# Three small moves around the dilated attention of a hybrid encoder layer: a weight load eight filler steps later, three more filler steps ahead of the attention, and a unit's low part in front of later maxima

## The chip, the cores and the metric

The kernel runs on one core of a Trainium2 chip. Its time is the device time of one execution in microseconds (us). Three executions of the kernel before took 1283.53, 1284.01 and 1286.13 us, so the median is 1284.01 us. One more execution was profiled.

The core's engines are TensorE (PE in the rows; PEld is its loading of weights), VectorE (DVE), ScalarE (ACT), GpSimd (POOL) and SyncE (SP), which in this kernel only issues DMA transfers, one after the other in a fixed order. Rows that are marked SPq are transfers of that queue.

## The reference, cut to what matters

One encoder layer over a sequence of 1024 tokens and a model width of 1024, batch 1. A normed input is projected once, and the projection is cut into the inputs of two attentions and of two gates:

```python
def hybrid_layer(x, positions, attn_norm_g, w_in, b_gate, ...):
    h = rmsnorm(x, attn_norm_g)
    proj = h @ w_in
    (c_q, c_kv, k_rope, z_mla, q_dil, k_dil, v_dil, z_dil,
     g_mla, g_dil) = jnp.split(proj, split_points, axis=-1)
    a_out = mla_attention(c_q, c_kv, k_rope, positions, ...)
    y_mla = (a_out * jax.nn.silu(z_mla)) @ w_o_mla
    d_out = dilated_mixture(q_dil, k_dil, v_dil, positions)
    y_dil = (d_out * jax.nn.silu(z_dil)) @ w_o_dil
    gate_mla = jax.nn.sigmoid(g_mla + b_gate[:D_MODEL])
    gate_dil = jax.nn.sigmoid(g_dil + b_gate[D_MODEL:])
    merged = gate_mla * y_mla + gate_dil * y_dil
    return x + merged @ w_out
```

The dilated mixture has 24 heads of width 64 in three groups of eight. A query of group 0 sees its neighbours up to 64 tokens away, one of group 1 every fourth token up to 256 away, one of group 2 every sixteenth up to 1024 away. Head i of the three groups is combined into one output, by the softmax over the groups of the logarithms of their denominators:

```python
    for g, (window, dilation) in enumerate(DIL_CONFIGS):   # (128,1), (512,4), (2048,16)
        out, lse = dilated_group(q[:, :, sl], k[:, :, sl], v[:, :, sl], dilation, window // (2 * dilation))
        ...
    alpha = jax.nn.softmax(jnp.stack(lses, axis=0), axis=0)
    out = jnp.sum(alpha[..., None] * outs, axis=0)
```

The latent attention (8 heads, all tokens see all) is `mla_attention`. After the layer there is a last norm.

## The kernel before, in words

**Stages.** Up to about 460 us of the span the kernel norms the input, projects it and rotates queries and keys. Queries, keys and values go to buffers in DRAM (`s_dq`, `s_dk`, `s_dv`), from which the attentions load them in the layout they need. From about 460 to 813 us runs the dilated attention, then the latent attention, and last the output projections. Products in full precision are made of three passes, high by high, low by high and high by low part of the operands (`mm3`, lines 77 to 79 in the rows).

**Fillers.** The projections of the gates (24 weight tiles of 128 columns: `zs` and `gt`, the list `ZG`) are not a stage of their own. They are a generator, `fillers`, that is advanced by one step at a time wherever the attention leaves room on TensorE. A weight tile has two halves of 512 tokens, a half has eight steps, and a step is one `mm3`, three products of 128 by 512. With the first step of a tile's first half goes the load of the weights of the tile after the next (`self.wload`, a transfer `w_raw<-wt` of 512 KB, line 634), with its fifth step the rounding of the next tile's weights into two parts (line 636: ScalarE's `CAST w_h`, GpSimd's `w_l`). After a half the result goes through a scaling on VectorE (`zg_z`, line 617), a tanh on ScalarE (lines 619 and 624), for `zs` two operations on GpSimd (lines 620 and 621), and a store of 256 KB (`s_zs<-zg_t` or `s_gt<-zg_t`). These parts (`after`) are advanced one at a time with every other step of the next half.

**Units.** The dilated attention works on four pairs of heads. A pair has five items: two heads of group 0, two of group 1, and both heads of group 2 together (the classes). A head has four units of 256 queries, the classes have two, so there are 18 units a pair and 72 in all. A unit has eight parts, called by `do(t, part)`: 0 scores (`s_ps`, lines 860 and 861 on TensorE), 1 maxima (line 870 on VectorE, two a unit, which also write the masked scores to `p`), 2 exponentials (line 877 on ScalarE), 3 transposes of the probabilities (line 884 on TensorE, into `pt`) and their rounding (`pt_h`, line 892 on ScalarE), 4 the low part (`pt_l`, line 896 on VectorE: `pt` minus `pt_h`), 5 the products with the values (`av`, lines 908 and 915 on TensorE, with the high and with the low part), 6 and 7 the copying out and adding up (line 934 on VectorE). An item's queries and keys (`op_b`, `op_a`) are loaded two items ahead, its values (`op_c`) one unit later.

**The loop.** It runs over t, and different units are at different parts in one turn. After the first two items' loads come `FIRST_FEED` filler steps on their own, and then in each turn:

```python
            do(t, 3)
            do(t + 2, 0)
            do(t + 2, 1)
            do(t, 4)
            ...
            self.feed(DIL_FEED[g])
            do(t - 2, 6)
            do(t + 2, 2)
            do(t - 2, 7)
            self.feed(DIL_FEED[g])
            do(t - 1, 5)
```

So the scores, maxima and exponentials run two units ahead of the transposes, and the products with the values one unit behind these. `feed` advances the fillers by 1.43 steps on the average, twice a turn; over the whole loop that makes 273 steps. After the loop, steps are taken until a half tile is whole (`while not self.whole`).

**Combining a pair.** When the last unit of a pair is through, `combine` spreads nine pieces of work over the next turns: the statistics go to DRAM and come back by token (`s_sd`, `c_sn`), differences, exponents and quotients are formed (`c_w`, `c_d`, lines 1100 to 1121), these factors go to DRAM (`s_rr<-c_w`) and come back spread over 64 partitions (`bc<-s_rr`, twelve transfers, 256 KB for two of them), and VectorE multiplies the three groups' sums by them (the weighted sums, line 1134), while GpSimd adds them up. The first of the spread tiles have five buffers; the last two transfers wait for one to come free.

**What sets the order.** From the start of the dilated attention to its end the order of the instructions on TensorE, VectorE, ScalarE and GpSimd is that in which the program calls them (`manual_schedule`). Before and after it a scheduler places the instructions, and the transfers in SP's queue that belong to earlier work are placed by it among the first transfers of the attention. Each engine then works off its own order, and waits where the next instruction's inputs or buffers are not ready.

Of the kernel before, what the change touches and what calls it, by code (L numbers as in the profile page):

```python
# [27 lines left out]
QK_SCALE = float(np.float32(96.0 ** -0.5))  # L28


FIRST_FEED = 19
DIL_FEED = (1.43, 1.43, 2.5, 2)
FEED = (0.95, 0.95)

# [12 lines left out]
def run_all(gen):  # L47
    while True:
        try:
            next(gen)  # L50
        except StopIteration as e:
            return e.value


class Net:
# [546 lines left out]
    def fillers(self):  # L602
# [3 lines left out]
        with tc.tile_pool(name="zt", reuse_waits="tile", bufs=2, side="right") as tp:  # L606
            z_tile = lambda: tp.tile([128, 512], F32, name="zg_z")
            t_tile = lambda: tp.tile([128, 512], F32, name="zg_t")
            tiles = ZG
# [17 lines left out]
            for n, i in enumerate(tiles):  # L627
                w = ahead
                for half in range(2):
                    ps = self.pj.tile([128, 512], F32, name="pj")  # L630
                    t = slice(half * 512, half * 512 + 512)
                    for kc in range(8):
                        self.mm3(ps, *self.at(w, kc), self.hTh[:, kc, t], self.hTl[:, kc, t], kc == 0, kc == 7)
                        if half == 0 and kc == 0 and n + 2 < len(tiles):
                            raw.append(self.wload(src(n + 2)))
                        if half == 0 and kc == 4 and n + 1 < len(tiles):
                            ahead = self.wtile(None, raw=raw.pop(0))

                        if kc % 2 == 0 and self.tail:
                            next(self.tail, None)  # L640
                        self.whole = kc == 7
                        if kc < 7:
                            yield
                    if self.manual:
                        self.tail = after(i, half, ps)
                    else:
                        self.tail = run_all(after(i, half, ps))
                    if self.dil_done and todo:
                        j, h2 = todo.pop(0)
                        self.piece(self.da, j, h2, 4 + j, self.brd, z_tile(), t_tile())  # L650
                    yield
# [15 lines left out]
        for dt in range(8):  # L667
            if dt % 2 == 0:
                w = self.wtile(a["wod"][dt // 2])
            for half in range(2):  # L670
                c = slice(512 * half, 512 * half + 512)
                t, ps = yield from self.o_proj(1, dt, half, w, dt % 2 * 4, range(4), self.brd, t_tile(), self.pj)
# [11 lines left out]
        for dt in range(8):  # L684
            if dt % 2 == 0:
                w = self.wtile(a["wom"][dt // 2], n=6)
            for half in range(2):
                c = slice(512 * half, 512 * half + 512)
                t, ps = yield from self.o_proj(0, dt, half, w, dt % 2 * 3, range(3), self.brm, t_tile(), self.pj)
# [323 lines left out]
    def dil_attention(self, ap, dx, pp):  # L1013

        items, units, ends = [], [], {}
        for pair in range(4):
            st, nums = {}, {}
            for g in range(2):
                for hh in range(2):
                    items.append(self.dil_head(pair, g, hh, st, nums, ap, dx, pp))  # L1020
            items.append(self.dil_classes(pair, st, nums, ap, dx, pp))
            ends[len(items) - 1] = self.combine(pair, st, nums, ap, dx, pp)
        for n, it in enumerate(items):
            for k, x in enumerate(it[2]):
                units.append((*x, n if k == len(it[2]) - 1 else None))
        for it in items[:2]:
            it[0]()
            it[1]()
        later = {}
        N = len(units)  # L1030

        def do(k, what):
            if 0 <= k < N:
                units[k][1 + what]()
        for _ in range(FIRST_FEED):
            next(self.fill)
        for t in range(-2, N + 11):
            g = units[min(max(t, 0), N - 1)][0] if t <= N else 3
            do(t, 3)
            do(t + 2, 0)  # L1040
            do(t + 2, 1)
            do(t, 4)
            if t + 2 < N:
                last = units[t + 2][-1]
                if last is not None and last + 2 < len(items):
                    items[last + 2][0]()
# [6 lines that stand above are left out]
            if 1 <= t <= N:  # L1053
                last = units[t - 1][-1]
                if last is not None:
                    if last + 2 < len(items):
                        items[last + 2][1]()
                    for k, f in ends.get(last, {}).items():
                        later.setdefault(t + 1 + k, []).append(f)
            for f in later.pop(t, []):  # L1060
                f()
# [318 lines left out]
```

## Time and profile before

| What | Value |
|---|---|
| Median of three executions | 1284.01 us (1283.53 to 1286.13) |
| Profiled execution, its own time | 1285.26 us |
| Its span in the profile | 1283.4 us |
| Mean granted clock of TensorE | 0.988 of full |
| TensorE busy | 1235.9 us, 96% of the span |
| VectorE, ScalarE, GpSimd busy | 755.8, 608.1, 506.6 us |
| DMA engines, main queue | 218.17 MB, 60.3% of 16 engines' span |
| The dilated attention | from about 460 to 813 us |

The profiled execution's own time is 1.86 us longer than its span, which begins with the first and ends with the last instruction that the profiler saw. A row of the timeline has the start, the length, the engine, the line in the kernel, the operation, the tile written and the tiles read, the shape and, at the end, how many instructions of the same kind in a row it stands for. A bracket behind it has the time for which the engine stood idle before the first of them, and what ended that idle time, by the profile. The clock is the share of full speed that the chip granted to TensorE. DMA share is the mean busy share of the core's 16 DMA engines.

### The profile page before, as it was taken

The numbers are of one execution on the slowest core, as the hardware profiler recorded it, in microseconds if no ns is written. First come the engines' busy times: TensorE is split into PE (matmuls) and PEld (weight loads), VectorE is DVE, ScalarE is ACT, GpSimd is POOL, SyncE is SP. The second block draws the span as 40 slices with busy tenths as digits, with TensorE's granted clock in tenths as the row PEclk, the third lists the DMA queues.
The fourth block names the chain that finished last, engine by engine and source line by source line (L and its number), as shares of the span: only waits on it lengthen the run. The fifth ranks groups of instructions, "written<-read, shape, count | busy, mean of one in ns | idle before, by whom it ended". The sixth has DMA issues, their size and how long they took to land.

```text
span 1283.4 us, 19686 instructions
## 1 busy us (share of the span) xinstructions
PE 1235.9 (96%) x6957; PEld 1072.8 (84%) x6957; DVE 755.8 (59%) x1368; ACT 608.1 (47%) x1276; POOL 506.6 (39%) x402
## 2 busy tenths in 40 slices
PE   8989999999999989998999999999999999997998
PEld 8989999888888868887888888887888888884886
DVE  7473526566566635566575663655556666669632
ACT  6533336443433426555554642455556555454322
POOL 2351219887777624526231132311112111246522
PEclk9989999999999999999999999999999999999999
DMA  9957583276456586978889796445437444236421
GB/s 321 258 168 270 219 295 132 99 189 168 119 139 163 123 215 182 212 195 222 211 215 231 187 241 163 150 131 149 113 93 199 117 119 129 70 112 208 145 97 68
DMA packets 134482, 219.43 MB, mean 171 GB/s; under 512 B 37160, under 2 KB 66672, under 8 KB 130480
## 3 DMA queue, kind: packets, MB, share of 16 engines
q1 hardware_dynamic: 134384, 218.17, 60.3%
q8 instruction: 55, 0.90, 0.3%
q14 instruction: 43, 0.35, 0.1%
HBM read 149.37 MB, written 68.75 MB: 170 GB/s over the span
## 4 chain that ended last, share of the span: by engine, by line
PE 65%; DMA 10%; issue 5%; DVE 5%; POOL 4%; ACT 2%; SPq 1%; DVEq 0%; ACTq 0%; POOLq 0%
PE pj L77 9%; PE pj L79 9%; PE pj L78 9%; PE pt L754 4%; PE av L763 2%; PE s_mla L77 2%; PE av L762 2%; PE s_mla L78 2%; PE s_mla L79 2%; DMA bc<-s_rr 2%; PE st_c L79 2%; PE st_c L77 2%; PE st_c L78 2%; PE st_d L78 2%; PE st_d L79 2%
## 5 line engine op out<-in xcount | busy, mean ns | idle before, releaser
L84 POOL TENSOR_TENSOR w_l<-w_raw,w_h 128x512 fp32r<-128x512 f32 (+1 forms) x176 | 227.4, 1305 | 411.7 <-ACT w_h L83 354.7
L77 PE MATMUL pj<-hT_h,w_h 128*128 128x512 f32 x384 | 156.5, 408 | 0.0
L79 PE MATMUL pj<-hT_h,w_l 128*128 128x512 f32 x384 | 152.3, 396 | 0.0
L78 PE MATMUL pj<-hT_l,w_h 128*128 128x512 f32 x384 | 152.1, 396 | 0.0
L83 ACT CAST w_h<-w_raw 128x512 fp32r<-128x512 f32 (+1 forms) x176 | 104.3, 615 | 84.5 <-POOL w_raw L427 72.8
L84 DVE TENSOR_TENSOR pt_l<-pt,pt_h 128x512 fp32r<-128x512 f32 x128 | 87.9, 688 | 66.1 <-ACT pt_h L83 65.2
L83 ACT CAST pt_h<-pt 128x512 fp32r<-128x512 f32 x128 | 74.6, 585 | 79.6 <-PE pt L754 47.8
L77 PE MATMUL pj<-w_h,hT_h 128*128 128x256 f32 x384 | 109.7, 286 | 0.0
L78 PE MATMUL pj<-w_l,hT_h 128*128 128x256 f32 x384 | 109.5, 285 | 0.0
L79 PE MATMUL pj<-w_h,hT_l 128*128 128x256 f32 x384 | 109.3, 285 | 0.0
L740 DVE TENSOR_REDUCE m_nm<-s_mla 128x1 f32<-128x1024 f32 x64 | 78.2, 1222 | 26.7 <-PE s_mla L79 26.1
L870 DVE CUSTOM_DVE_ANT_0 p<-s_ps,masks 128x256 f32<-128x256 f32 x128 | 48.9, 419 | 69.8 <-PE s_ps L861 59.7
L877 ACT ACTIVATE p<-p,d_st 128x256 f32<-128x256 f32 x128 | 64.1, 502 | 51.3 <-DVE d_st L870 51.2
L79 PEld LDWEIGHTS pj<-hT_h,w_l 128*128 128x128 f32 x384 | 73.0, 190 | 15.9
L78 PEld LDWEIGHTS pj<-hT_l,w_h 128*128 128x128 f32 x384 | 73.3, 191 | 11.4
L77 PEld LDWEIGHTS pj<-hT_h,w_h 128*128 128x128 f32 x384 | 73.4, 191 | 11.2
L743 ACT ACTIVATE p<-s_mla,m_nm 128x1024 f32<-128x1024 f32 x64 | 71.8, 1122 | 18.2 <-PE pt L754 17.3
L754 PE MATMUL pt<-consts,p 128*128 128x128 f32 x512 | 78.1, 272 | 1.7 <-ACT p L743 1.7
L77 PEld LDWEIGHTS pj<-w_h,hT_h 128*128 128x128 f32 x384 | 74.2, 193 | 0.9
L78 PEld LDWEIGHTS pj<-w_l,hT_h 128*128 128x128 f32 x384 | 74.2, 193 | 0.8
L79 PEld LDWEIGHTS pj<-w_h,hT_l 128*128 128x128 f32 x384 | 74.2, 193 | 0.8
L762 PE MATMUL av<-pt_h,op_c 128*128 128x256 f32 x256 | 68.8, 289 | 0.0
(307 smaller groups left out, 3319.3 us busy)
## 6 DMA issues: line engine op xcount, KB each, us to landing
w_raw<-wt SPq DMA_DIRECT2D x48, 512.0 KB, 3.6
op_b<-s_dq SPq DMA_DIRECT2D x32, 512.0 KB, 8.0
gate<-s_gt SPq DMA_DIRECT2D x43, 256.0 KB, 3.0
s_dq<-dq_st SPq DMA_DIRECT2D x80, 128.0 KB, 2.4
s_dk<-dq_st SPq DMA_DIRECT2D x80, 128.0 KB, 2.4
s_dv<-dv_st SPq DMA_DIRECT2D x32, 256.0 KB, 4.3
s_gt<-zg_t SPq DMA_DIRECT2D x32, 256.0 KB, 3.8
w_raw<-wv SPq DMA_DIRECT2D x12, 512.0 KB, 5.2
```

Of the source, the lines that this page charges most:

```text
L77: mm(out, lh, rh, start=start, stop=False, skip_group_check=skip)
L78: mm(out, lh, rl, start=False, stop=False, skip_group_check=skip)
L79: return mm(out, ll, rh, start=False, stop=stop, skip_group_check=skip)
L83: self.nc.scalar.copy(out=h, in_=raw)
L84: sub.tensor_tensor(out=l, in0=raw, in1=h.bitcast(F32), op=ALU.subtract)
L740: v.tensor_reduce(out=nm[:, hh, qb:qb + 1], in_=s, axis=AX.X, op=ALU.max, negate=True)
L743: nc.scalar.activation(out=p, in_=s, func=AF.Exp, bias=nm[:, hh, qb:qb + 1], accum_out=den[:, hh, qb:qb + 1])
L754: self.anchor = nc.tensor.transpose(pt[:, o:o + 128], P[b2][:, 128 * kc:128 * kc + 128], self.ident)
L762: nc.tensor.matmul(a_out, vv[:, kc], ph[:, s], start=kc == 0, stop=False)
L763: nc.tensor.matmul(a_out, vv[:, kc], pl[:, s], start=False, stop=kc == 7)
L870: nc.vector.tensor_tensor_reduce(out=p[:, c], in0=x["s"][:, c], in1=mask, op0=ALU.add, op1=ALU.min, scale=-0.125, scalar=3e38, accum_out=s ...
L877: nc.scalar.activation(out=p, in_=p, func=AF.Exp, scale=-1.0, bias=nm, accum_out=den)
```

## The change

There are three edits.

- `FIRST_FEED` is 22 and no longer 19: three more filler steps stand ahead of the first unit's scores. All later filler steps stand three steps earlier against the units, which is about one turn of the loop (2 times 1.43 steps). The number of steps of the stage, 19 + 273 = 292, used to be filled up to 296 by four steps after the loop; now it is 22 + 273 = 295 and one.
- In `fillers` the load of the third tile's weights (n is 0 there, and `src(n + 2)` the third tile) goes with the first step of the first tile's second half, eight steps later. For all other tiles the condition says what it said.
- In the loop the low part of unit t (part 4) is called ahead of the maxima of unit t + 2 (part 1).

```diff
-FIRST_FEED = 19
+FIRST_FEED = 22
...
                     for kc in range(8):
                         self.mm3(ps, *self.at(w, kc), self.hTh[:, kc, t], self.hTl[:, kc, t], kc == 0, kc == 7)
-                        if half == 0 and kc == 0 and n + 2 < len(tiles):
+                        if half == (n == 0) and kc == 0 and n + 2 < len(tiles):
                             raw.append(self.wload(src(n + 2)))
                         if half == 0 and kc == 4 and n + 1 < len(tiles):
                             ahead = self.wtile(None, raw=raw.pop(0))
...
             do(t, 3)
             do(t + 2, 0)
+            do(t, 4)
             do(t + 2, 1)
-            do(t, 4)
```

Three places show what this makes of the order. The first is SP's queue around the start of the dilated attention, before the change and after it. `op_c` are the values of the second item, `w_raw` of the first such row is the load of the third tile's weights, `s_dk2` are the last stores of keys of the stage before, and `s_zs` the fillers' first store. The number behind a name is the buffer's.

```order
L73 DMA op_a_4807<-s_dk0_65 64x1152 x2
L73 DMA op_c_4812<-s_dv0_68 128x9x128
L73 DMA w_raw_4821<-wt 128x1024
L73 DMA s_dk2_67<-dq_st00_4743 32x1024 x4
L73 DMA s_dk2_67<-dq_st10_4744 32x1024 x4
L73 DMA s_zs_71<-zg_t_4857 128x512
L73 DMA w_raw_4888<-wt 128x1024
```

```order
L73 DMA op_a_4807<-s_dk0_65 64x1152 x2
L73 DMA op_c_4812<-s_dv0_68 128x9x128
L73 DMA w_raw_4854<-wt 128x1024
L73 DMA s_dk2_67<-dq_st00_4743 32x1024 x4
L73 DMA s_dk2_67<-dq_st10_4744 32x1024 x4
L73 DMA s_zs_71<-zg_t_4857 128x512
L73 DMA w_raw_4888<-wt 128x1024
```

The third tile's load is a later one by its number, but stands at the same place: behind the loads of the second item and ahead of the last eight stores of keys.

The second place is VectorE's order at the first units of the first head, before and after. The rows of line 870 are the maxima of a unit (two, each with the reading of its result), line 896 is a low part and line 617 a filler's scaling.

```order
L870 ISA p,d_st<-s_ps,masks 128x256
L870 ISA d_st 128x1
L870 ISA p,d_st<-s_ps,masks 128x256
L870 ISA d_st 128x1
L896 TENSOR_TENSOR pt_l<-pt,pt_h 128x512
L617 TENSOR_TENSOR zg_z<-pj,R 128x512
L870 ISA p,d_st<-s_ps,masks 128x256
```

```order
L617 TENSOR_TENSOR zg_z<-pj,R 128x512
L896 TENSOR_TENSOR pt_l<-pt,pt_h 128x512
L870 ISA p,d_st<-s_ps,masks 128x256
L870 ISA d_st 128x1
L870 ISA p,d_st<-s_ps,masks 128x256
L870 ISA d_st 128x1
L896 TENSOR_TENSOR pt_l<-pt,pt_h 128x512
```

The low part moved from behind the two maxima of the unit two further on to ahead of them, and the filler's scaling, three steps earlier, from behind the low part to one turn ahead.

The third place is SP's queue where the factors of the second pair are spread. The rows are a piece of the difference, `s_rr` are the factors on their way to DRAM, `bc` their spreading, and `w_raw` and `s_gt` belong to the fillers.

```order
 L73 DMA op_a<-s_dk_66 64x1024 x2
+L73 DMA s_gt<-zg_t 128x512
 L73 DMA s_rr<-c_w 16x6x64
-L73 DMA s_gt<-zg_t 128x512
+L73 DMA w_raw<-wt 128x1024
 L73 DMA bc<-s_rr 64x512 x10
-L73 DMA w_raw<-wt 128x1024
 L73 DMA op_c<-s_dv_69 128x8x128
 L73 DMA bc<-s_rr 64x512 x2
```

The fillers' store moved from behind the factors to ahead of them, and the fillers' weight load from behind the first ten spreading transfers to ahead of these. At the other pairs the fillers' stores and loads move by as much: at the first pair two stores and a weight load come ahead of the loads of the next items, at the third a weight load comes ahead of the loads of keys and a store ahead of the factors, and at the last a store comes between the first ten spreading transfers and the last two, with the weight loads around it earlier by one place.

## The prediction

> **What bounds the kernel now.** I read the page's busy shares, then the dilated stage by stretches, then TensorE's own idle time in that stage, row by row, and last the queues that end each wait.
>
> ```profile
> PE 1235.9 (96%) x6957; PEld 1072.8 (84%) x6957; DVE 755.8 (59%) x1368; ACT 608.1 (47%) x1276; POOL 506.6 (39%) x402
> 460.00:780.00 320.00, 303.79 (x1840) 267.97 (x1839) 188.62 (x491) 171.71 (x441) 111.02 (x100) 0.98 0.85 210
> ```
>
> TensorE sets the end: it is busy for 96% of the span. The second row (length, then busy time of PE, PEld, DVE, ACT, POOL, then the granted clock, the DMA share, GB/s) is the dilated stage, which all three edits touch: 320 us, of which PE works 303.8, so some 16 us are idle, while the DMA engines are 85% busy at 210 GB/s. The timeline of PE has that idle time in few places (start, length of the first, the work, and in brackets the idle time and what ended it):
>
> ```profile
> 480.24 1.18 PE L884 MATMUL pt<-consts,p 128*128 128x128 f32 x4 [5.48 <-ACT p L877]
> 590.70 0.38 PE L915 MATMUL av<-pt_l,op_c 128*128 128x256 f32 x1 [1.09 <-DVE pt_l L896]
> 600.32 0.38 PE L915 MATMUL av<-pt_l,op_c 128*128 128x256 f32 x1 [2.45 <-DVE pt_l L896]
> 674.46 0.39 PE L915 MATMUL av<-pt_l,op_c 128*128 128x256 f32 x1 [2.36 <-DVE pt_l L896]
> 691.42 0.36 PE L860 MATMUL s_ps<-op_a,op_b 128*128 128x256 f32 x1 [2.00 <-DMA op_a<-s_dk]
> 743.00 0.39 PE L915 MATMUL av<-pt_l,op_c 128*128 128x256 f32 x1 [1.59 <-DVE pt_l L896]
> 751.22 0.38 PE L915 MATMUL av<-pt_l,op_c 128*128 128x256 f32 x1 [1.05 <-DVE pt_l L896]
> ```
>
> These make 16.0 us: 5.5 before the first unit, and 10.5 around the three places where a pair of heads is combined. A stall also costs clock:
>
> ```profile
> 480.24:484.60 4.36, 4.36 (x14) 3.60 (x15) 2.40 (x8) 4.00 (x14) 3.87 (x4) 0.50 0.54 180
> 600.80:604.30 3.50, 3.50 (x15) 3.11 (x14) 2.97 (x11) 2.92 (x9) 0.45 (x1) 0.51 0.87 284
> 676.00:679.30 3.30, 3.30 (x10) 2.52 (x9) 3.30 (x12) 2.93 (x9) 1.04 (x2) 0.50 0.96 338
> 691.50:694.90 3.40, 3.40 (x17) 2.89 (x18) 2.03 (x6) 1.09 (x4) 0.84 (x1) 1.00 0.95 185
> ```
>
> After the stalls of 5.48, 2.45 and 2.36 us the clock is at a half for 4.36, 3.5 and 3.3 us, so 2.2, 1.7 and 1.7 us are lost; after the one of 2.00 us it stays at 1.00. All of it together, 16 + 5.6, is what can be won in this stage, and the edits aim at pieces of it.
>
> **The later load of the third tile.** In the queue of SP the load stands where it stood: behind the first six loads of the attention, ahead of the last eight stores of keys, in both programs. What it loads, when it may start and what waits behind it are the same. Its consumer, ScalarE's rounding at the fifth filler step of the second tile, is the same step too. So 0.
>
> **Three more steps ahead.** What ends the first stall:
>
> ```profile
> 457.25 0.39 PE L77 MATMUL pj<-hT_h,w_h 128*128 128x512 f32 x1
> 457.93 0.39 PE L77 MATMUL pj<-hT_h,w_h 128*128 128x512 f32 x1
> 465.79 10.80 SPq L73 DMA_DIRECT2D s_dk<-dq_st  x8
> 479.11 0.42 DVE L870 CUSTOM_DVE_ANT_0 p<-s_ps,masks 128x256 f32<-128x256 f32 x1 [10.10 <-DMA s_dk<-dq_st]
> ```
>
> One filler step takes 457.93 - 457.25 = 0.68 us, three take 2.04. The first maxima wait for the last stores of keys (their buffers lie where the probabilities go), which SP issues from 465.79 on for 10.8 us. Nothing in that chain is moved, so the units begin at 480.24 as before; the three steps run inside the stall, which falls from 5.48 to 3.44 us. The stage's number of steps is rounded up to whole half tiles: 19 + 273 = 292 became 296 with four steps of padding, 22 + 273 = 295 becomes 296 with one. So the 2.04 us come off at the end of the stage, and whether they are won is decided there:
>
> ```profile
> 809.71 0.69 DVE L1134 TENSOR_TENSOR num<-num,bc 128x512 f32<-128x512 f32 x1 [1.32 <-DMA bc<-s_rr]
> 810.92 2.54 DVE L740 TENSOR_REDUCE m_nm<-s_mla 128x1 f32<-128x1024 f32 x2
> 813.19 0.19 ACT L743 ACTIVATION_READ_ACCUMULATOR p<-s_mla,m_nm 128x1 f32 x1
> 813.43 0.44 PE L754 MATMUL pt<-consts,p 128*128 128x128 f32 x2
> ```
>
> The first transposes of the latent attention start 0.05 us after its first probabilities are ready (813.19 + 0.19), and these wait for VectorE, which comes straight from the last weighted sums of the last pair. PE, 2.04 us early, would stand and wait for them. What can come forward is that chain on VectorE, by as much as the filler's scalings in it no longer wait for PE; the order has one of them now ahead of the denominators, and on SP a gate store ahead of the last spreading, which ends the wait at 809.71; both take part of that back. I take -0.3, between -2.04 (chain fully earlier) and +1.25 (the store's 256 KB at the 210 GB/s above, in full).
>
> The clock at the start: 3.44 us is still longer than the stalls of 2.36 and 2.45 that halved it, so I take a loss of 1.7 in place of 2.2: -0.5, between -2.2 (no halving) and 0.
>
> The Trainium skill ("TensorE: Matmul & The Clock Gate", "Why this matters for your kernels") says to keep idle gaps of TensorE under about 3 us, since one idle window of some 3.4 us halves the clock. For this stall it agrees with what I took from the rows: 3.44 is still too long. For the stalls of 2.45 and 2.36 us the trace differs (0.51 and 0.50), and I go by the trace; by the page's limit the new short stalls below would cost no clock, and the sum would be -3.8 in place of -2.8.
>
> **The low part ahead of the maxima.** At the waits for pt_l VectorE comes late out of a weighted sum, and then works off its queue. At the second one:
>
> ```profile
> 598.90 0.41 DVE L870 CUSTOM_DVE_ANT_0 p<-s_ps,masks 128x256 f32<-128x256 f32 x1
> 599.59 0.68 DVE L896 TENSOR_TENSOR pt_l<-pt,pt_h 128x512 fp32r<-128x512 f32 x1
> 599.36 0.51 ACT L877 ACTIVATE p<-p,d_st 128x256 f32<-128x256 f32 x1 [4.12 <-DVE d_st L870]
> 599.86 0.49 ACT L877 ACTIVATE p<-p,d_st 128x256 f32<-128x256 f32 x1
> 600.47 0.59 ACT L892 CAST pt_h<-pt 128x512 fp32r<-128x512 f32 x1
> 600.78 1.00 PE L884 MATMUL pt<-consts,p 128*128 128x128 f32 x4
> ```
>
> Now: two maxima from 598.90, the low part from 599.59 to 600.27, PE goes on at 600.32. With the low part first it is done 0.69 earlier, and the four products start at 599.63. But 0.46 us of work later (600.78 - 600.32) PE is at the transposes of the next unit, which need the exponentials behind those maxima. The maxima, 0.60 later, make the second exponential end at 600.95 in place of 600.35, and with the read of its sum at about 601.05, where the second transpose now goes between 600.78 and 601.03 (a quarter of its row's 1.00 later). So PE loses up to 0.25 us in place of winning 0.69, and I take the whole, since the other two places have the faster transposes of a full clock: the wait changes its name from pt_l to p. One such place per pair counts, the last: 3 x 0.25 = +0.75, between -2.1 and +2.1 (0.69 each way). Elsewhere the low part has two units of lead, and no wait is there to be shortened.
>
> **Where the fillers' transfers fall.** Each filler event comes about one unit earlier against the units, and with it its place on SP. Bytes are priced by the 210 GB/s above: a 512 KB weight tile 2.5 us, a 256 KB store 1.25.
>
> ```profile
> SPq L73 <- POOL zg_t L621: 5.4, 1, 5.4
> 583.84 6.21 SPq L73 DMA_DIRECT2D bc<-s_rr  x10
> 605.78 1.22 SPq L73 DMA_DIRECT2D op_a<-s_dk  x2
> 606.36 1.26 POOL L620 TENSOR_TENSOR zg_t<-zg_t,zg_z 128x512 f32<-128x512 f32 x1
> 615.85 0.35 PE L860 MATMUL s_ps<-op_a,op_b 128*128 128x256 f32 x1
> ```
>
> Pair 0: a store that waits 5.4 us for GpSimd holds the spreading of the factors (bc) until 583.84. Now the store one earlier stands ahead of s_rr, and nothing between s_rr and bc; the spreading starts perhaps 1.2 us earlier. But behind it the next store stands ahead of the loads of pair 1's first head, on GpSimd's product for it (now at 606.36; one unit earlier, some 603.5). These loads land about 8 us after their issue, shortly before PE needs them at 615.85. The store's 1.25 us and SP's wait come on top. I set the two against each other: 0, between -3.5 (both waits of the pair) and +3.5.
>
> ```profile
> DMA  9999999997999999898303755769999999999989
> 664.11 0.53 SPq L73 DMA_DIRECT2D w_raw<-wt  x1
> 672.13 0.99 DVE L1134 TENSOR_TENSOR num<-num,bc 128x512 f32<-128x512 f32 x1 [3.18 <-DMA bc<-s_rr]
> 679.96 1.23 SPq L73 DMA_DIRECT2D op_a<-s_dk  x2
> ```
>
> Pair 1: the first row is the DMA engines' busy share from 635 to 680 us in 40 slices; they idle around 655 and are full from 665 on. The weight tile issued at 664.11 stands in that full stretch, ahead of the last spreading, which ends the wait at 672.13, and of the keys of 679.96, which end PE's wait at 691.42. It now goes between s_rr and bc, into the idle slices: 2.5 us less in both queues. -2.5, between -4.4 (both waits gone) and 0 (it delays the spreading instead).
>
> ```profile
> DMA  0048999999970099999899940353564799999999
> 735.33 5.16 SPq L73 DMA_DIRECT2D bc<-s_rr  x7
> ```
>
> Pair 2, from 705 to 755 us: s_rr is issued at about 729, and bc can only start at 735.33, when the full stretch before it is through. The weight tile in it moves ahead of the loads, into the two empty slices; a store comes in: -2.5 + 1.25 = -1.25, between -2.64 and 0.
>
> **Clock again.** The stalls of pairs 0 and 1 get shorter, but what they gave in clock is taken by the loads that PE meets next. New stalls of 1.5 to 3 us are to be expected ahead of pair 1 and ahead of the latent attention: I take one halving of 1.7 at six chances in ten, +1.0, between 0 and +3.4.
>
> **Sum.** -0.3 - 0.5 + 0.75 + 0 - 2.5 - 1.25 + 1.0 = -2.8 us. The profiled execution took 1285.26 us (its span 1283.4 and 1.9 around it), 1.25 above the median of the runs shown, 1284.01. So it would take 1282.5, and the median is forecast at **1281.2 us**, with 1278.5 to 1284 as this case's own range.
>
> **Rivals.** (1) *The balloon*: at 85% and with stretches that are full, every wait won is paid at the next transfer that is late anyway. For it: 674.46 and 691.42 are ended by one backlog. Against it: the idle slices exist. What is left is -0.8, and half a microsecond to either side: 1283.2; if the store ahead of pair 1's loads blocks SP in full, 1286. (2) *A tight loop between ScalarE and VectorE* (slower): with the low part first, the rounding of a unit (0.59), its low part (0.68), the maxima until the first exponential (0.46) and both exponentials with their reads (1.1) follow each other, 2.8 us, and ScalarE's next rounding stands behind them. Two neighbouring units:
>
> ```profile
> 516.82 0.60 PE L884 MATMUL pt<-consts,p 128*128 128x128 f32 x4
> 520.29 0.60 PE L884 MATMUL pt<-consts,p 128*128 128x128 f32 x4
> ```
>
> A unit takes 3.5 us here, so the loop fits, unless ScalarE puts a weight tile's casts (128x1024, twice a unit's rounding: an estimate of 1.2 us) into it. It decides from the point where the lead of two units is used up; then some 11 units with casts (one per 16 steps at 2.86 steps a unit) cost 0.5 each: +5.5 with the rest won only by half, 1288. Against it: the lead is never touched now, except at the first unit. (3) *All of it*: the chain at the end comes forward in full (-2.04), and of the 10.5 us around the pairs two thirds go: 1275. For it: each place's queue gets shorter somewhere. (4) *The edits do nothing*: true of the load, not of the others.
>
> **How the numbers follow.** The forecast 0.45, the balloon 0.27, the loop 0.14, all of it 0.14. What this kernel's timing can tell from no change is about 0.2%, 2.6 us: faster means under 1281.4, slower over 1286.6. Of the forecast's case somewhat over half is under 1281.4 (0.26), with all of it (0.14) and a little of the balloon (0.04): 0.44. The balloon's late loads (0.06) and the loop (0.14): 0.20. The rest, 0.36, is no change. The range takes in most of (3) and the loop's price: 1275.5 to 1288.
>
> **What would show it.** Right: the first stall 3.4 us with the first maxima still at 479; PE's waits for pt_l gone or named p; the wait at 691 under half a microsecond or moved; a stall of 1 to 2 us ahead of the latent attention's first transposes. Wrong: units starting before 480; no stall at the latent attention (then rival 3); waits of PE on p within a pair, away from the weighted sums (the loop); a wait for keys at the first unit of pair 1 over 2 us (the balloon).

## The result, and the profile after

The change makes the kernel slower: 1294.17 us (median of five, 1291.10 to 1298.12) against 1285.59 us for the kernel before (five, 1283.53 to 1286.43), a ratio of 1.0071 with a 95% interval of 1.0051 to 1.0091. The profiled execution took 1294.66 us, its span is 1292.9 us.

The page's busy times and the dilated stage in the view by stretches, for the changed kernel:

```profile
PE 1241.5 (96%) x6957; PEld 1076.1 (83%) x6957; DVE 758.2 (59%) x1368; ACT 609.9 (47%) x1276; POOL 507.3 (39%) x402
```

```profile
460.00:780.00 320.00, 303.19 (x1818) 265.82 (x1817) 191.28 (x490) 172.97 (x442) 111.71 (x100) 0.98 0.84 207
```

TensorE is 5.6 us longer busy with the same number of instructions: its mean granted clock is 0.984, where it was 0.988. In the stage it does less in the same 320 us (1818 instructions, 1840 before).

TensorE's own idle time, from the timeline of the changed kernel in the dilated stage (all stalls over 0.3 us; the last row, without one, is the first transposes of the latent attention):

```profile
480.14 1.18 PE L884 MATMUL pt<-consts,p 128*128 128x128 f32 x4 [2.58 <-ACT p L877]
540.98 0.36 PE L860 MATMUL s_ps<-op_a,op_b 128*128 128x256 f32 x1 [1.47 <-DMA op_a<-s_dk]
599.07 0.39 PE L915 MATMUL av<-pt_l,op_c 128*128 128x256 f32 x1 [1.76 <-DVE pt_l L896]
600.04 1.39 PE L884 MATMUL pt<-consts,p 128*128 128x128 f32 x4 [0.34 <-ACT p L877]
620.38 0.56 PE L860 MATMUL s_ps<-op_a,op_b 128*128 128x256 f32 x1 [5.10 <-DMA op_a<-s_dk]
672.16 0.33 PE L884 MATMUL pt<-consts,p 128*128 128x128 f32 x1 [0.41 <-ACT p L877]
680.49 0.33 PE L884 MATMUL pt<-consts,p 128*128 128x128 f32 x1 [0.35 <-ACT p L877]
697.31 0.36 PE L860 MATMUL s_ps<-op_a,op_b 128*128 128x256 f32 x1 [3.45 <-DMA op_a<-s_dk]
756.88 0.33 PE L884 MATMUL pt<-consts,p 128*128 128x128 f32 x1 [0.35 <-ACT p L877]
819.53 0.80 PE L77 MATMUL pj<-hT_h,w_h 128*128 128x512 f32 x1 [3.36 <-DVE zg_z L617]
822.25 0.63 PE L754 MATMUL pt<-consts,p 128*128 128x128 f32 x2
```

The waits for `pt_l` are nearly all gone, and short ones for `p` stand in their place. What is new are two waits for keys (540.98 and 620.38) and one for a filler's scaling ahead of the latent attention (819.53); the wait for the fourth pair's keys has grown from 2.00 us to 3.45 (697.31). Where the time of these two executions parts can be read from four instructions that stand in both traces, and from the end:

| | before | after | later by |
|---|---|---|---|
| first transposes of the dilated stage | 480.24 | 480.14 | -0.10 |
| first scores of the third pair | 615.85 | 620.38 | 4.53 |
| first scores of the fourth pair | 691.42 | 697.31 | 5.89 |
| first transposes of the latent attention | 813.43 | 822.25 | 8.82 |
| end of the span | 1283.4 | 1292.9 | 9.5 |

How far two executions of one order can differ is shown by the load's edit alone (first section of the experiments), whose order is that of the kernel before: from the first transposes of the stage to those of the latent attention its trace has 339.43 us, where the kernel before has 333.19 and the changed kernel 342.11. So a later row of this table says less than an earlier one: up to the third pair's first scores they have 135.21, 135.61 and 140.24 us, in the same order.

(The prediction calls the loads issued at 605.78 those of pair 1's first head; counted from one, they are the third pair's.) The clock behind four of the stalls after the first, in the view by stretches:

```profile
599.07:602.50 3.43, 3.07 (x12) 2.48 (x13) 1.97 (x6) 2.71 (x7) 2.19 (x3) 0.60 0.86 170
620.38:624.00 3.62, 3.62 (x11) 3.08 (x12) 1.46 (x6) 1.92 (x6) 0.24 (x1) 0.55 1.00 221
697.31:701.00 3.69, 3.69 (x14) 3.04 (x15) 2.06 (x7) 1.53 (x5) 0.00 (x0) 0.69 1.07 236
819.53:823.00 3.47, 3.47 (x9) 2.75 (x10) 2.20 (x2) 3.04 (x5) 1.75 (x2) 0.50 0.72 273
```

That is 1.4, 1.6, 1.1 and 1.7 us lost to the clock (length times one minus the clock).

**The keys of the third pair.** SP's waits between 596 and 612 us (in total, times, longest):

```profile
SPq L73 <- POOL zg_t L621: 6.0, 1, 6.0
```

And the rows around it in the timeline of SP and of GpSimd:

```profile
606.21 0.32 SPq L73 DMA_DIRECT2D s_zs<-zg_t  x1
609.37 1.23 SPq L73 DMA_DIRECT2D op_a<-s_dk  x2
...
603.53 1.29 POOL L620 TENSOR_TENSOR zg_t<-zg_t,zg_z 128x512 f32<-128x512 f32 x1
604.90 1.28 POOL L621 TENSOR_TENSOR zg_t<-zg_t,zg_z 128x512 f32<-128x512 f32 x1
```

SP stands for 6.0 us at one store (the fourteenth of `zs`), until GpSimd's second operation for it is over (604.90 + 1.28 = 606.18). Behind it stand the third pair's loads; the keys are issued at 609.37, where it was 605.78 before. So the keys are issued 3.59 us later, and TensorE waits 5.10 us.

**The end of the stage.** VectorE and ScalarE in the last combining, after the change:

```profile
794.02 0.87 DVE L1102 TENSOR_TENSOR c_w<-c_w,c_sn 16x128 f32<-16x128 f32 x3
797.21 0.69 DVE L617 TENSOR_TENSOR zg_z<-pj,R 128x512 f32<-128x512 f32 x1 [2.32 <-PE pj L79]
799.10 0.88 DVE L1112 TENSOR_TENSOR c_d<-c_w,c_sn 16x128 f32<-16x128 f32 x3 [1.20 <-ACT c_w L1105]
799.91 1.38 DVE L1113 TENSOR_TENSOR c_d<-c_d 16x128 f32<-16x128 f32 x1
818.79 0.68 DVE L617 TENSOR_TENSOR zg_z<-pj,R 128x512 f32<-128x512 f32 x1
...
797.94 0.72 ACT L624 ACTIVATE zg_t<-zg_z,consts 128x512 f32<-128x512 f32 x1 [4.72 <-DVE zg_z L617]
798.57 0.51 ACT L1105 ACTIVATE c_w<-c_w 16x384 f32<-16x384 f32 x1
```

And the same place before:

```profile
789.47 0.87 DVE L1102 TENSOR_TENSOR c_w<-c_w,c_sn 16x128 f32<-16x128 f32 x3
790.92 0.87 DVE L1112 TENSOR_TENSOR c_d<-c_w,c_sn 16x128 f32<-16x128 f32 x3 [0.59 <-ACT c_w L1105]
791.72 0.27 DVE L1113 TENSOR_TENSOR c_d<-c_d 16x128 f32<-16x128 f32 x1
```

Before, the denominators (L1112) begin 1.45 us after the last differences (L1102). After, a filler's scaling has come between them. It waits for TensorE's half tile until 797.21, its tanh stands ahead of the exponents on ScalarE, and the denominators begin 5.08 us after the differences. The differences themselves are 4.55 us late (794.02, before 789.47), and the last weighted sum begins 8.31 us late (818.02, before 809.71). A scaling stands behind it on VectorE (818.79), and TensorE waits for the buffer that this scaling empties (819.53). The longer gap comes with the steps ahead and not by chance: it is 5.08 to 5.35 us in the three traces with 22 steps and the order of the combining as it was, 4.38 with 20 steps, and 1.45 to 1.47 in all others.

### The profile page after: what moved, and what is told of

The parts are those of the page before. It is cut to its first block, busy times and chain, and to the rows that moved or that the text cites. A ratio compares the mean times of both kernels' runs of the same rounds, so it can differ in the third digit from the quotient of the medians.

```text
span 1292.9 us, 19675 instructions
## 1 busy us (share of the span) xinstructions
PE 1241.5 (96%) x6957; PEld 1076.1 (83%) x6957; DVE 758.2 (59%) x1368; ACT 609.9 (47%) x1276; POOL 507.3 (39%) x402
## 5 line engine op out<-in xcount | busy, mean ns | idle before, releaser
L84 DVE TENSOR_TENSOR pt_l<-pt,pt_h 128x512 fp32r<-128x512 f32 x128 | 88.0, 688 | 67.6 <-ACT pt_h L83 66.7
L896 DVE TENSOR_TENSOR pt_l<-pt,pt_h 128x512 fp32r<-128x512 f32 x64 | 44.0, 688 | 66.7 <-ACT pt_h L892 66.5
```

What stands on the lines that cost most here:

```text
L84: sub.tensor_tensor(out=l, in0=raw, in1=h.bitcast(F32), op=ALU.subtract)
L896: nc.vector.tensor_tensor(out=l, in0=x["pt"], in1=h.bitcast(F32), op=ALU.subtract)
```

## The experiments

Each was timed against the kernel before on the same chip; the kernel before had medians of 1285.10 (first four), 1285.64 (next four), 1286.73 (next three) and 1285.66 us (last). Single executions spread by several us to either side, so ratios are given with their 95% intervals. The changed kernel was not timed again beside them; where a version is compared with it, the two ratios to the kernel before are set against each other, and 0.1% is 1.3 us.

### The three edits alone

```diff
-FIRST_FEED = 19
+FIRST_FEED = 22
```

> The kernel before with only the 22 filler steps ahead of the attention. SP's queue stands exactly as in the changed kernel. Theory (the later keys come from where the fillers' stores and loads stand in SP's queue): it holds nearly all of the loss, 1292 to 1295 us, with a wait for keys near 620 us of some 5 us and a wait of some 3 us ahead of the latent attention. Rival (the low part in front of the maxima makes the loss, the tight loop): 1284 to 1287. Rival (the two together make it): about half, 1289 to 1290.

1291.13 us, ratio 1.0044 (1.0027 to 1.0062): the largest part of the loss, 0.44% of 0.71%. The long waits are those of the whole change, in the timeline of this kernel:

```profile
613.32 0.55 PE L860 MATMUL s_ps<-op_a,op_b 128*128 128x256 f32 x1 [5.93 <-DMA op_a<-s_dk]
689.73 0.55 PE L860 MATMUL s_ps<-op_a,op_b 128*128 128x256 f32 x1 [3.20 <-DMA op_a<-s_dk]
812.48 0.79 PE L77 MATMUL pj<-hT_h,w_h 128*128 128x512 f32 x1 [4.56 <-DVE zg_z L617]
```

The time missed the expected 1292 by 0.9 us, and the interval takes in both "nearly all" and the rival of "about half". The waits at the keys and ahead of the latent attention are the expected ones.

```diff
+            do(t, 4)
             do(t + 2, 1)
-            do(t, 4)
```

> The kernel before with only the low part in front of the maxima. SP's queue stands exactly as in the kernel before, and only VectorE's order differs. Theory: the waits for the low part at the weighted sums shrink by 0.3 to 0.7 us each and partly turn into waits for the exponentials; half of it is given back at the next keys: 1284 to 1285.5. Rival (tight loop): 1288 to 1293, with waits for the exponentials inside a pair.

1286.90 us, ratio 1.0017 (1.0000 to 1.0034): between no change and 4.4 us slower, above what was expected. In its timeline the waits for the low part are shorter, waits for `p` of 0.35 to 0.42 us have come, and there are waits for keys:

```profile
615.17 0.36 PE L860 MATMUL s_ps<-op_a,op_b 128*128 128x256 f32 x1 [2.28 <-DMA op_a<-s_dk]
692.02 0.55 PE L860 MATMUL s_ps<-op_a,op_b 128*128 128x256 f32 x1 [2.52 <-DMA op_a<-s_dk]
```

At 615 us the kernel before had no wait in its trace. That TensorE waits at the keys for what it won at the weighted sum is not shown by it, though: the next run, with the order of the kernel before, waits there as well. No wait for `p` stands away from the weighted sums, so the tight loop did not occur.

```diff
-                        if half == 0 and kc == 0 and n + 2 < len(tiles):
+                        if half == (n == 0) and kc == 0 and n + 2 < len(tiles):
```

> The kernel before with only the third tile's load called eight steps later. No engine's order differs from before. Theory: no change, 1285.6 within 1 us. Rival (the load's place matters): a change of more than 2 us.

1286.13 us, ratio 0.9998 (0.9979 to 1.0017): no change. Its order is that of the kernel before, so its trace shows how far waits vary from one execution to the next. At the third pair's keys, where the kernel before had none, it has 2.86 us:

```profile
611.45 0.36 PE L860 MATMUL s_ps<-op_a,op_b 128*128 128x256 f32 x1 [2.86 <-DMA op_a<-s_dk]
```

TensorE came to these scores early here; they begin 135.21 us after the stage's first transposes, 135.61 in the kernel before. Measured so, the third pair's first scores tell the versions apart where the length of the wait does not: 134.1 to 136.9 us in the ten traces in which the keys' loads stand ahead of the store or the store is on another queue, and 137.2 to 140.2 in the four in which the store stands ahead of them (the changed kernel, the steps alone, and two runs below).

### The store ahead of the keys

In the changed kernel the one store is held back until the second step of the next half tile:

```diff
-                    self.dma(self.zs[i][:, c], t)
+                    if (i, half) == (2, 1):
+                        self.held = [(self.zs[i][:, c], t)]
+                    else:
+                        self.dma(self.zs[i][:, c], t)
...
+                        if kc == 1:
+                            for x in self.held:
+                                self.dma(*x)
+                            self.held = []
```

> The changed kernel, with one store of 256 KB (the fourteenth of zs, which waits for GpSimd until 606.2 us) called a few filler steps later, so that it stands behind the third pair's first keys in SP's queue and no longer ahead of them. Theory (this one store holds the keys): the keys are issued about 3.6 us earlier, the wait of 5.10 us at 620 us falls under 1.5 us and its half clock goes, 1286.5 to 1289.5 us. Rival (the full DMA engines make the keys late, whatever stands ahead of them): the wait stays over 4 us and the time within 1 us of 1294.

1286.02 us, ratio 1.0012 (0.9995 to 1.0030): 0.59%, some 7.6 us, under the changed kernel with its 1.0071 (1.0051 to 1.0091), by moving a single transfer of 256 KB. Its SP queue and the wait (line numbers are eight higher here):

```profile
604.12 1.23 SPq L73 DMA_DIRECT2D op_a<-s_dk  x2
605.44 0.53 SPq L73 DMA_DIRECT2D s_zs<-zg_t  x1
...
613.02 0.35 PE L868 MATMUL s_ps<-op_a,op_b 128*128 128x256 f32 x1 [1.11 <-DMA op_a<-s_dk]
810.00 0.80 PE L77 MATMUL pj<-hT_h,w_h 128*128 128x512 f32 x1 [3.44 <-DVE zg_z L617]
```

The wait of 5.10 is 1.11 us, and the scores begin 136.21 us after the stage's first transposes, where the changed kernel has 140.24. The gain is at the upper end of the 4.7 to 7.7 us that were expected. The last row shows what is left: the wait ahead of the latent attention still stands, at 3.44 us, and yet the interval of the ratio takes in no change. One expected step came out smaller: counted from the same transposes the keys are issued after 127.31 us in place of 129.23, 1.9 us earlier and not 3.6, since SP now waits 3.4 us for TensorE among the loads of queries.

The reverse in the kernel before: only the loads of this one head are called after the first fillers of their turn, so that the store stands ahead of them.

```diff
-                if last is not None and last + 2 < len(items):
+                if last is not None and last + 2 < len(items) and last != 8:
                     items[last + 2][0]()
             self.feed(DIL_FEED[g])
+            if t + 2 < N and units[t + 2][-1] == 8:
+                items[10][0]()
```

> The kernel before, with the queries and keys of the third pair's first head called after the first filler steps of their turn, so that one store of zs (which waits for GpSimd until 609.0 us) stands ahead of them in SP's queue, as in the changed kernel; nothing else moves. Theory (this order alone makes the wait): the keys are issued about 3.5 us later, PE waits 4 to 6 us for them, and the time rises by 4 to 7 us, to 1289 to 1292. Rival (it needs the three earlier steps too): within 1.5 us of 1285.

1291.31 us, ratio 1.0040 (1.0015 to 1.0064): the median is 5.7 us over that of the kernel before in the same runs. The store waits as in the changed kernel, and so do the keys:

```profile
606.34 0.33 SPq L73 DMA_DIRECT2D s_zs<-zg_t  x1
607.90 1.23 SPq L73 DMA_DIRECT2D op_a<-s_dk  x2
...
616.82 0.36 PE L860 MATMUL s_ps<-op_a,op_b 128*128 128x256 f32 x1 [3.79 <-DMA op_a<-s_dk]
```

So this order alone makes a loss, of 0.15 to 0.64%, without any further filler step ahead. The wait came out just under the expected 4 to 6 us.

### The last combining

In the changed kernel the last pair's exponents and denominators are called with its differences, one turn earlier:

```diff
-        return {-1: statistics, 0: by_token, 3: differences, 4: lambda: (exponents(), factors()), 5: quotients,
+        early = {3: lambda: (differences(), exponents(), factors())} if pair == 3 else {3: differences, 4: lambda: (exponents(), factors())}
+        return {-1: statistics, 0: by_token, **early, 5: quotients,
```

> The changed kernel, with the exponents and denominators of the last pair called in one go with its differences, one turn earlier, so that no filler's scaling and tanh stand between them on VectorE and ScalarE. SP's queue stands as in the changed kernel. Theory (the wait of 3.36 us ahead of the latent attention comes from the last combining, which waits for a filler's half tile in its middle): the factors are ready 3 to 5 us earlier, that wait falls under 0.5 us with its half clock, and the time falls by 4 to 5 us from 1294, to 1289 to 1290. Rival (the spreading transfers set the end, behind the stores): the wait stays over 2 us and the time over 1292.

1289.71 us, ratio 1.0041 (1.0021 to 1.0060): 0.30%, some 3.9 us, under the changed kernel, but the two intervals overlap, so this gain is only just clear of noise. The denominators come 1.47 us after the differences again, and the stall of 3.36 us is one of 0.68:

```profile
791.47 0.87 DVE L1102 TENSOR_TENSOR c_w<-c_w,c_sn 16x128 f32<-16x128 f32 x3
792.94 0.88 DVE L1112 TENSOR_TENSOR c_d<-c_w,c_sn 16x128 f32<-16x128 f32 x3 [0.59 <-ACT c_w L1105]
...
816.16 0.44 PE L754 MATMUL pt<-consts,p 128*128 128x128 f32 x2 [0.68 <-ACT p L743]
```

Both repairs together (the two diffs above):

> The changed kernel with both: the fourteenth zs store behind the third pair's first keys, and the last pair's exponents and denominators called with its differences. Theory: the gains of the two add up, 1280 to 1282.5 us, faster than the kernel before. Rival (each win is paid at the next transfer that is late): 1285 to 1287, no better than with the store alone.

1284.31 us, ratio 1.0009 (0.9989 to 1.0030): the kernel before again, and 0.62%, some 8.0 us, under the changed kernel. The gains of 0.59 and 0.30% would make 0.89; with intervals of 0.2% on each ratio it is not shown that they fail to add up. What is seen is that the early denominators on top of the store's move brought nothing that can be told from none (1.0012 to 1.0009). In its profile 2.58 and 3.46 us are waited for the keys of the third and the fourth pair.

### Twenty steps, and the rest

```diff
-FIRST_FEED = 22
+FIRST_FEED = 20
```

> The changed kernel with 20 filler steps ahead of the attention and no longer 22. At the first three pairs SP's queue then differs from before only in that a store of each comes one to seven places earlier, and all stores stand behind the keys that wait for none; at the last pair it differs as with 22. Theory (what counts is which store stands ahead of which keys, not the number of steps): no wait over 2.5 us for keys near 615, 1284 to 1287.5. Rival (the loss grows with the number of steps): about a third of it, 1288 to 1289, with a wait of some 3 us for keys.

1289.27 us, ratio 1.0040 (1.0015 to 1.0066), a median above both the range of the theory and that of its rival. Its interval (1287.6 to 1294.1 us) takes in the rival's range and not the theory's. The wait it was about is gone, as the order of the stores said: 0.45 us at the third pair's keys. The other two remain:

```profile
617.53 0.35 PE L860 MATMUL s_ps<-op_a,op_b 128*128 128x256 f32 x1 [0.45 <-DMA op_a<-s_dk]
695.82 0.55 PE L860 MATMUL s_ps<-op_a,op_b 128*128 128x256 f32 x1 [3.66 <-DMA op_a<-s_dk]
821.41 0.79 PE L77 MATMUL pj<-hT_h,w_h 128*128 128x512 f32 x1 [2.25 <-DVE zg_z L617]
```

The profiled execution took 1297.41 us, 8 us over the median, so where the last microseconds of the median lie can't be read from it. This run counts against the store as the whole account: the loss by its median is that of the run above with the keys behind the store, and no store holds the third pair's keys here.

Both repairs, with the third edit taken back:

```diff
-            do(t, 4)
             do(t + 2, 1)
+            do(t, 4)
```

> The kernel of both (store behind the keys, last pair's denominators early), with the low part again behind the maxima: the three steps ahead and the two repairs without the third edit. Theory (the low part in front only turns waits for pt_l into waits for p and for keys): within 2 us of the kernel with it, 1283 to 1286. Rival (the low part in front costs 1.5 to 2 us, as it seemed when it was alone): 1282 to 1282.8.

1283.56 us, ratio 0.9982 (0.9960 to 1.0005). The same with the low part in front had 1.0009 (0.9989 to 1.0030); the intervals overlap, so the third edit costs little or nothing here, as was expected.

The fillers' stores on other queues than SP's, first in the kernel before:

```diff
-                    self.dma(self.zs[i][:, c], t)
+                    nc.gpsimd.dma_start(out=self.zs[i][:, c], in_=t)
...
-                    yield self.dma(self.gt[i - 8][:, c], t)
+                    yield nc.scalar.dma_start(out=self.gt[i - 8][:, c], in_=t)
```

> The kernel before, with the fillers' stores issued by the engines that make their data (zs on GpSimd's queue, gt on ScalarE's) and no longer on SP's. SP then waits for no filler ahead of any load. Theory (what a store costs is the queue that waits behind it): keys are issued earlier at every pair, the wait near 691 us shrinks, 1279 to 1283. Rival (the DMA engines' load sets when keys land, or issuing costs the other engines as much): 1284 to 1290.

1289.60 us, ratio 1.0039 (1.0015 to 1.0062): slower, against the theory. No store stands ahead of the third pair's keys, and yet:

```profile
605.69 1.23 SPq L73 DMA_DIRECT2D op_a<-s_dk  x2
...
616.51 0.55 PE L860 MATMUL s_ps<-op_a,op_b 128*128 128x256 f32 x1 [3.57 <-DMA op_a<-s_dk]
```

The keys are issued when they were in the kernel before (605.78), and TensorE begins with them at 616.51, where it was 615.85. It had come to them at 612.94, 2.9 us earlier than before, and that came to nothing. Why the whole is slower, and not the same, stays open.

Then the changed kernel with these queues and the last pair's denominators early:

> The changed kernel with the last pair's denominators early and the fillers' stores on the queues of GpSimd and ScalarE; the fourteenth zs store is not moved otherwise. Theory (the wait of 5 us near 620 us is SP standing at that store): the wait falls under 2 us without the store being called later, and the time is at or under that of the kernel before on the same stores, 1279 to 1283. Rival: the wait stays over 4 us, 1288 to 1291.

1283.11 us, ratio 0.9980 (0.9959 to 1.0002), 0.1 us over what was expected. The wait of 5.10 us is 1.97 here, though the store is called where the change puts it, and the scores begin 134.98 us after the stage's first transposes: what delayed the keys was SP standing at the store.

And the same without the third edit (the two calls exchanged again, as above):

> The three steps ahead, the last pair's denominators early and the fillers' stores on the queues of GpSimd and ScalarE, with the low part behind the maxima as in the kernel before. Theory (waits for keys pace the stage, and the low part's place only names the wait differently): within 1.5 us of the same with the low part in front, 1282 to 1285 beside a kernel before at 1285 to 1287. Rival (the low part in front is what makes the stores' queues pay): 1287 to 1290.

1283.41 us, ratio 0.9981 (0.9963 to 1.0000). Of four versions with the wait at the store and the one in the combining repaired, three (these two and the one with 0.9982) lie about 0.2% under the kernel before and one at 1.0009, each with an interval that reaches to no change. A version that clearly beats the kernel before was not found.

## Why the prediction was wrong, point by point

- **The later load, 0**: right, 0.9998 when alone.
- **Three more steps ahead, -0.5**: right in the stall, not shown in the clock. The stall fell from 5.48 to 2.58 us (3.44 was forecast), and the first transposes stand at 480.14 in place of 480.24. Over the traces with the stores on SP's queue it is 4.52 to 5.48 us with 19 steps and 2.58 to 3.46 with 22, on the average 2.0 us less, as forecast (the one trace with 20 steps has 5.91). The clock over the next 4.4 us is higher by a tenth:

```profile
480.14:484.50 4.36, 4.36 (x16) 3.58 (x17) 1.23 (x4) 2.52 (x8) 4.28 (x5) 0.61 0.55 180
```

  But with the load's edit alone, 19 steps and a stall of 4.52 us, it is 0.62 over the 4.3 us behind that stall, so the half microsecond agrees by luck as far as the runs show.

- **The low part, +0.75**: the wait changes its name from `pt_l` to `p`, as forecast, with 0.34 to 0.41 us per place where up to 0.25 was taken. Alone it came to between 0 and 4.4 us (1.0000 to 1.0034); with the two repairs it could not be told from nothing. That a win of TensorE there is waited for at the next keys would explain it, and is not shown.
- **Pair 0, 0**: this is the step that failed first. It named the store ahead of the keys and GpSimd's operation for it, and then priced the place as if the store were released at 603.5, which is where the first of GpSimd's two operations begins. The second ends at 606.18. So the loads were held 2.7 us longer than counted, and the earlier spreading that was set against it came 0.91 us earlier (582.93 to 583.84 before), with the wait for `pt_l` after it still 1.76 us. It also took these loads to land 8 us after their issue, with some 2 us to spare. That is the median of the loads of queries in the kernel before (8.0 us); for keys of this size (288 KB) it is 10.0, so that 605.78 + 10.0 is 615.8, when TensorE was at them: there was nothing to spare. The bound of +3.5 also left out the halved clock behind a long wait. Measured: 4.53 us by the third pair's first scores and 1.6 more by the clock; 0.40% of the time, 5.7 us by the medians, when the order is made in the kernel before, and 0.59%, some 7.6 us, when it is undone.
- **Pair 1, -2.5**: its wait of 2.36 for `pt_l` and the halved clock behind it went, as forecast. But the weight tile between `s_rr` and `bc` was not free of cost in the emptier stretch. Before, the spreading began 3.55 us after the factors were issued, and now 4.52 us after that; SP's wait for the factors to reach DRAM went from 2.7 to 3.6 us:

```profile
660.15 0.33 SPq L73 DMA_DIRECT2D s_rr<-c_w  x1
660.57 0.38 SPq L73 DMA_DIRECT2D w_raw<-wt  x1
664.67 6.20 SPq L73 DMA_DIRECT2D bc<-s_rr  x10
```

  And before:

```profile
654.26 0.33 SPq L73 DMA_DIRECT2D s_rr<-c_w  x1
657.81 6.20 SPq L73 DMA_DIRECT2D bc<-s_rr  x10
```

  And the wait for the fourth pair's keys rose from 2.00 to 3.45 us with a clock of 0.69 behind it. The balloon, a rival, is the better account of this place, as an argument: no run took this weight tile alone.
- **Pair 2, -1.25**: waits of 1.59 and 1.05 us became one of 0.35 us. Right in kind, a little too small.
- **The end, -0.3**: failed. From the fourth pair's first scores to the latent attention's first transposes the table has 2.93 us more (8.82 less 5.89), outside the bounds of -2.04 and +1.25. The part that moved the scaling among the denominators was seen in the order, and was priced as a little of the gain given back. It is a chain over two engines that a filler's half tile was put into: 5.08 against 1.45 us between differences and denominators, and 1.7 us of clock behind the wait at its end. The mechanism is shown, its price only roughly. Over that stretch the traces with 22 steps and the stores on SP's queue have 124.6 to 125.5 us with the late denominators and 120.9 to 121.8 with the early ones, so 3 to 4 us; but two executions of the order of before have 122.0 and 125.9. By the times, the early denominators gave some 3.9 us in the changed kernel, and nothing measurable once the store was moved.
- **Clock again, +1.0**: one halving at six chances in ten. There were four partial or full ones behind later stalls, 5.8 us, against 3.4 us before at the weighted sums that went away.
- **The rivals**: the tight loop, which was to be the slower side, did not occur: no wait for `p` stands away from the weighted sums. The balloon was nearest: it named the store, and its sign, a wait over 2 us for the keys of this pair, came (5.10 us). But its 1286 was the price of the store without the clock and without the end. By its name it says that every win is paid again; what the runs show is rather one place where SP stood still.

The Trainium skill ("TensorE: Matmul & The Clock Gate", "Why this matters for your kernels") has idle gaps of some 3 us as what costs clock. The wait of 1.76 us at 599.07, with 0.34 more behind it, was followed by 0.60 for 3.4 us; here the trace differs again.

What stays open: the loss with the stores off SP in the kernel before, the loss with twenty steps, and whether the two repairs give less together than apart.

## What to carry to other kernels

A store in an in-order DMA queue costs what waits behind it: release it at the end of the last operation that writes its data, and then list the loads that stand behind it and who needs them first. A filler's step that slips into a serial chain on a second engine lengthens the chain by the filler's own wait for its input, however short its work is. Where two paths arrive together (here TensorE, and the keys through one queue), a win on one of them can come back as a wait for the other: TensorE was at the keys 2.9 us earlier in one run here, and began with them no earlier. And the length of a wait in one trace is a poor measure of a delay: one order had no wait and one of 2.86 us at the same keys in two executions. Measure from an event ahead of both paths.

## What the runs showed of the hardware that was not expected

An addition of 16x128 on VectorE took 1.38 us (799.91), where the same took 0.27 us before (791.72), and the next one (801.32) 1.26 us in place of 0.28. GpSimd was at the rounding of a weight tile at that time:

```profile
799.66 2.78 POOL L84 TENSOR_TENSOR w_l<-w_raw,w_h 128x512 fp32r<-128x512 f32 x2 [8.82 <-ACT w_h L83]
```

That GpSimd is what slowed them was not tested. They did not make this chain longer as a whole, since a scaling and slower products stood in it before: from the denominators to the store of the factors it has 5.49 us, and had 5.91. The Trainium skill ("SBUF — State Buffer", "SBUF: two separate sides") says that a VectorE operation with two inputs in SBUF and a GpSimd operation that reads SBUF exclude each other for a whole instruction. The rows agree with it: both additions and `w_l` have two inputs, and each addition took about as long as one of the two GpSimd operations beside it (2.78 us for two).

And the length of a stall did not settle the clock behind it: it stayed at 1.00 after 2.00 us in the kernel before, and fell to 0.60 after 1.76 and 0.34 us.
